# A 3x3 convolution of 16 images on one core: images paired across the partitions, and two output rows that share a product

## The chip, the cores and the metric

The kernel runs on one core of one Trainium2 chip. The metric is the device time of the kernel in microseconds (us), as the median of several runs. A profile of one execution goes with it: what each engine did and when, and what the DMA engines moved. The engines are TensorE (PE in the profile; its loads of weights are listed apart as PEld), VectorE (DVE), ScalarE (ACT), GpSimd (POOL) and SyncE (SP), whose only work here is to issue transfers.

## What is computed

The input `x` has 16 images of 64 channels and 64 x 64 pixels, the weight 128 output channels by 64 input channels by 3 x 3, both in fp32. The output is the convolution with a border of zeros, in fp32, 128 channels per image:

```python
x_pad = np.pad(x, ((0, 0), (0, 0), (1, 1), (1, 1)))
for b, co, ci, kh, kw in all_indices:          # 16, 128, 64, 3, 3
    if weight[co, ci, kh, kw] != 0:
        output[b, co] += weight[co, ci, kh, kw] * x_pad[b, ci, kh:kh+64, kw:kw+64]
```

Nine tenths of the weights are zero, at random places. Neither kernel makes use of it: both multiply with the full 64 x 128 matrix of each of the nine taps. The input is 16.8 MB, the output 33.6 MB.

## The kernel before

Each image is cut into an upper and a lower half of 32 rows. The 64 channels of the upper half lie in partitions 0 to 63, those of the lower half in 64 to 127, each with one more row at the cut (33 rows), so that the row is loaded twice. Loads are issued by GpSimd and turn fp32 into bf16 on the way. Images 1 to 14 are loaded two at a time.

```python
xs_group = xg_pool.tile([128, 2, XROWS, W], BF16, name="xsg")      # 3 buffers; XROWS = 33
nc.gpsimd.dma_start(                                                # line 107
    out=xs_group[0:64]...,   in_=x[b : b + 2, :, 0:XROWS, :]...)
nc.gpsimd.dma_start(                                                # line 111
    out=xs_group[64:128]..., in_=x[b : b + 2, :, H - XROWS : H, :]...)
```

A unit is 8 rows of the upper half and the same 8 of the lower one. For each of the nine taps there are two matmuls, one for each half: 64 channels against 8 x 64 pixels, with a 64 x 128 weight. The two use different rows of the array and different PSUM tiles. The nine taps add up in PSUM, and the sum is copied to SBUF by VectorE or ScalarE.

```python
for ui, (ur0, rb) in enumerate(units):
    ...                                       # psums: one [128, rb, 64] fp32 tile for each half
    for idx, (kh, kw) in enumerate(POS_ORDER):          # nine taps
        for half in range(2):
            ...                               # rows and columns of this tap, cut at the border
            nc.tensor.matmul(                           # line 175
                psum_t[:, rel_lo:rel_hi, j_lo:j_hi],
                wT[pbase : pbase + 64, kh * KW + kw, :],
                xs[idx_rhs],
                start=(idx == 0), stop=(idx == len(POS_ORDER) - 1),
            )
    if not streamed:
        for half in range(2):
            nc.any.tensor_copy(out=oimg[:, r0:r1, :], in_=psums[half])     # line 186
    else:                                     # images 13 to 15
        nc.vector.tensor_copy(...)                      # line 188
        nc.scalar.copy(...)                             # line 191
        ...                                   # store of these rows, 512 KB
```

Images 2 to 11 are stored in pairs of 4 MB, images 0, 1 and 12 alone, and images 13 to 15 unit by unit. The weights come in fp32, are cast to bf16 by VectorE, and are transposed with 18 matmuls against an identity (line 84).

Of the kernel before, what the change touches and what calls it, by code (L numbers as in the profile page):

```python
# [1 line left out]

# [5 lines left out]

FP32 = mybir.dt.float32  # L10
BF16 = mybir.dt.bfloat16


POS_ORDER = [(1, 1), (1, 0), (1, 2), (0, 0), (0, 1), (0, 2), (2, 0), (2, 1), (2, 2)]
CHUNK_ORDER = [1, 0, 2]


@with_exitstack
def kernel(
# [6 lines left out]
    nc = tc.nc  # L26

    B, C_IN, H, W = x.shape
    C_OUT, C_IN2, KH, KW = weight.shape
    assert (C_IN, H, W) == (64, 64, 64) and (C_OUT, KH, KW) == (128, 3, 3)  # L30

    HALF = H // 2
    XROWS = HALF + 1
    SPLIT = 10

    SINGLE_OUT = {0, 1, 12}
    PAIR_OUT_START = {2, 4, 6, 8, 10}
    STREAM_OUT = {13, 14, 15}
    UNITS_8 = [(r, 8) for r in range(0, HALF, 8)]
    STREAM_UNITS = {  # L40
        13: UNITS_8,
        14: UNITS_8,
        15: [(0, 8), (8, 8), (16, 8), (24, 4), (28, 4)],
    }

    const_pool = ctx.enter_context(tc.tile_pool(name="const", bufs=1))
    x0_pool = ctx.enter_context(tc.tile_pool(name="x0", bufs=2))
    xg_pool = ctx.enter_context(tc.tile_pool(name="xg", bufs=3))
    outs_pool = ctx.enter_context(tc.tile_pool(name="osb", bufs=3))
    outg_pool = ctx.enter_context(tc.tile_pool(name="osbg", bufs=2))  # L50
    psum_pool = ctx.enter_context(tc.tile_pool(name="psum", bufs=8, space=bass.MemoryType.PSUM))

    xs0 = x0_pool.tile([128, XROWS, W], BF16, name="xs0")
    nc.gpsimd.dma_start(out=xs0[0:64, 0:SPLIT], in_=x[0, :, 0:SPLIT, :])  # L54
    nc.gpsimd.dma_start(  # L55
        out=xs0[64:128, 0:SPLIT], in_=x[0, :, H - XROWS : H - XROWS + SPLIT, :]
    )
    nc.gpsimd.dma_start(out=xs0[0:64, SPLIT:XROWS], in_=x[0, :, SPLIT:XROWS, :])  # L58
    nc.gpsimd.dma_start(  # L59
        out=xs0[64:128, SPLIT:XROWS], in_=x[0, :, H - XROWS + SPLIT : H, :]  # L60
    )

    w_sb = const_pool.tile([C_OUT, C_IN * KH * KW], FP32)
    nc.sync.dma_start(out=w_sb, in_=weight.rearrange("o i kh kw -> o (i kh kw)"))
    w_sb3 = w_sb.rearrange("o (i k) -> o i k", k=KH * KW)

    w_bf = const_pool.tile([C_OUT, C_IN * KH * KW], BF16)
    w_bf3 = w_bf.rearrange("o (i k) -> o i k", k=KH * KW)
    for kh in CHUNK_ORDER:
        nc.vector.tensor_copy(  # L70
            out=w_bf3[:, :, kh * KW : (kh + 1) * KW],
            in_=w_sb3[:, :, kh * KW : (kh + 1) * KW],
        )

    ident = const_pool.tile([128, 128], BF16)
    make_identity(nc, ident)

    wT = const_pool.tile([128, KH * KW, C_OUT], BF16)
    for kh in CHUNK_ORDER:
        wps = psum_pool.tile([128, 4, 128], FP32, name="psum_t")  # L80
        for j in range(KW):
            sl = w_bf3[:, :, kh * KW + j]
            for half in range(2):
                nc.tensor.matmul(  # L84
                    wps[half * 64 : (half + 1) * 64, j, :],
                    sl,
                    ident,
                    start=True,
                    stop=True,
                )  # L90
        nc.scalar.copy(out=wT[:, kh * KW : kh * KW + KW, :], in_=wps[:, 0:KW, :])  # L91

    xs_group = None
    oimg_pair = None

    for b in range(B):
        if b == 0:
            xs = xs0
            xsel = ()
        elif b == B - 1:  # L100
            xs = x0_pool.tile([128, XROWS, W], BF16, name="xs15")
            nc.gpsimd.dma_start(out=xs[0:64], in_=x[b, :, 0:XROWS, :])  # L102
            nc.gpsimd.dma_start(out=xs[64:128], in_=x[b, :, H - XROWS : H, :])  # L103
            xsel = ()
        elif b % 2 == 1:
            xs_group = xg_pool.tile([128, 2, XROWS, W], BF16, name="xsg")
            nc.gpsimd.dma_start(  # L107
                out=xs_group[0:64].rearrange("i n r c -> i n (r c)"),
                in_=x[b : b + 2, :, 0:XROWS, :].rearrange("n i r c -> i n (r c)"),
            )  # L110
            nc.gpsimd.dma_start(  # L111
                out=xs_group[64:128].rearrange("i n r c -> i n (r c)"),
                in_=x[b : b + 2, :, H - XROWS : H, :].rearrange(
                    "n i r c -> i n (r c)"
                ),
            )
            xs = xs_group
            xsel = (0,)
        else:
            xs = xs_group  # L120
            xsel = (1,)

        if b in SINGLE_OUT or b in STREAM_OUT:
            oimg = outs_pool.tile([C_OUT, H, W], FP32, name="oimg")
        elif b in PAIR_OUT_START:
            oimg_pair = outg_pool.tile([C_OUT, 2, H, W], FP32, name="oimg2")
            oimg = oimg_pair[:, 0]
        else:
            oimg = oimg_pair[:, 1]

        streamed = b in STREAM_OUT
        if streamed:
            oimg_blk = oimg.rearrange("o (blk r) c -> o blk r c", blk=2)
            out_blk = out[b].rearrange("o (blk r) c -> o blk r c", blk=2)
            units = STREAM_UNITS[b]
        else:
            units = UNITS_8

        for ui, (ur0, rb) in enumerate(units):
            psums = []  # L140
            infos = []
            for half in range(2):
                r0 = half * HALF + ur0
                r1 = r0 + rb
                start_row = 0 if half == 0 else H - XROWS
                pbase = half * 64
                psum_t = psum_pool.tile([128, rb, W], FP32, name="psum_t")
                psums.append(psum_t)
                infos.append((r0, r1, start_row, pbase))

            for idx, (kh, kw) in enumerate(POS_ORDER):
                di, dj = kh - 1, kw - 1
                for half in range(2):
                    r0, r1, start_row, pbase = infos[half]
                    psum_t = psums[half]

                    i_lo = max(r0, -di)
                    i_hi = min(r1, H - di)
                    j_lo = max(0, -dj)
                    j_hi = min(W, W - dj)  # L160

                    rel_lo, rel_hi = i_lo - r0, i_hi - r0
                    xr_lo = i_lo + di - start_row
                    xr_hi = i_hi + di - start_row
                    xc_lo, xc_hi = j_lo + dj, j_hi + dj

                    idx_rhs = (slice(pbase, pbase + 64),) + xsel + (
                        slice(xr_lo, xr_hi),
                        slice(xc_lo, xc_hi),
                    )  # L170
                    rhs = xs[idx_rhs]
                    out_ap = psum_t[:, rel_lo:rel_hi, j_lo:j_hi]
                    lhsT = wT[pbase : pbase + 64, kh * KW + kw, :]

                    nc.tensor.matmul(  # L175
                        out_ap,
                        lhsT,
                        rhs,
                        start=(idx == 0),
                        stop=(idx == len(POS_ORDER) - 1),  # L180
                    )

            if not streamed:
                for half in range(2):
                    r0, r1, _, _ = infos[half]
                    nc.any.tensor_copy(out=oimg[:, r0:r1, :], in_=psums[half])  # L186
            else:
                nc.vector.tensor_copy(  # L188
                    out=oimg[:, infos[0][0] : infos[0][1], :], in_=psums[0]
                )  # L190
                nc.scalar.copy(  # L191
                    out=oimg[:, infos[1][0] : infos[1][1], :], in_=psums[1]
                )
                src = oimg_blk[:, :, ur0 : ur0 + rb, :]
                dst = out_blk[:, :, ur0 : ur0 + rb, :]
                if ui % 2 == 0:
                    nc.sync.dma_start(out=dst, in_=src)
                else:
                    nc.scalar.dma_start(out=dst, in_=src)  # L199

        if b in SINGLE_OUT:
            nc.sync.dma_start(out=out[b], in_=oimg)
        elif (b - 1) in PAIR_OUT_START:
            nc.sync.dma_start(
                out=out[b - 1 : b + 1].rearrange("n o h w -> o n (h w)"),
                in_=oimg_pair.rearrange("o n h w -> o n (h w)"),
            )


# [28 lines left out]
```

## Time and profile before

| | |
|---|---|
| time, median of 3 runs | 137.39 us (137.11 to 138.22) |
| span of the profiled execution | 136.1 us |
| moved by DMA, as it lands | 42.67 MB |
| read from HBM | 17.60 MB |
| written to HBM | 33.55 MB |
| instructions of TensorE | 1188 matmuls, 1188 loads of weights |

In the profile, a group of instructions is written as line, engine, operation, what it writes, `<-`, what it reads, with the shapes, the count, the total busy time and the mean time of one in ns. After the second bar stands how long the engine sat idle just before these instructions, and what it then had waited for. Rows of digits cut the span into 40 equal slices; a 9 means 90% busy or more. "DMA" in such a row is the mean busy share of the core's 16 DMA engines. The busy times of matmuls overlap, since two run at once. L175 is line 175 of the kernel, and the same line serves all products of the convolution.

### The profile page before, as it was taken

The page shows a single profiled execution, that of the slowest core. Times are in us where ns is not written, and L with a number is a line of the kernel's source. Part 1 is how long each engine was busy: PE and PEld are TensorE (multiplying, and loading weights), DVE is VectorE, ACT ScalarE, POOL GpSimd, SP SyncE. Part 2 cuts the span into 40 slices and gives each one's busy share as a digit, 9 for nine tenths or more (in the row PEclk, how much of TensorE's full clock was granted, in tenths as well). Part 3 has the DMA queues.
Part 4 walks back from the last instruction along what each step waited for, and adds up shares of the span by engine and source line. Part 5 has one row for each costly group of instructions (what it writes and reads, how often), then busy time and mean ns, then how long its engine had stood idle before and what let it go on. Part 6 is the DMA issues. An engine that isn't in the chain of part 4 may idle for free.

```text
span 136.1 us, 2653 instructions
## 1 busy us (share of the span) xinstructions
PE 126.7 (93%) x1188; PEld 77.1 (57%) x1188; DVE 45.2 (33%) x68; ACT 40.2 (30%) x69; POOL 12.2 (9%) x26
## 2 busy tenths in 40 slices
PE   0699999999999999999999999999999999999960
PEld 0555666666565656665656655665656655656650
DVE  0203432344234432343234423443244333443240
ACT  3302332233323332233223332333233323332230
POOL 6950000003000110003000110000000000000000
PEclk9999999999999999999999999999999999999999
DMA  4999999999999999999999999999509999999884
GB/s 104 119 189 211 216 229 350 363 342 363 245 226 409 443 338 195 302 416 443 274 205 393 438 395 228 294 405 455 231 10 462 385 453 409 389 404 393 329 326 157
DMA packets 7980, 42.67 MB, mean 313 GB/s; under 512 B 673, under 2 KB 1313, under 8 KB 6305
## 3 DMA queue, kind: packets, MB, share of 16 engines
q1 hardware_dynamic: 3840, 30.97, 55.6%
q0 software_dynamic: 2496, 8.65, 33.4%
q10 hardware_dynamic: 1632, 2.88, 5.6%
q8 instruction: 9, 0.15, 0.4%
q14 instruction: 3, 0.02, 0.0%
HBM read 17.60 MB, written 33.55 MB: 376 GB/s over the span
## 4 chain that ended last, share of the span: by engine, by line
PE 92%; POOL 2%; issue 1%; ACT 1%; ACTq 0%; POOLq 0%
PE psum_t L175 91%; PE psum_t L84 1%; ACT oimg L191 1%; POOL xs L54 0%; ACTq L199 0%; POOL xs L55 0%; POOL xsg L107 0%; POOL xs L58 0%; POOL ident masks.py:199 0%; POOL ident masks.py:197 0%; POOL xs L59 0%; POOLq masks.py:199 0%; POOLq L222 0%
## 5 line engine op out<-in xcount | busy, mean ns | idle before, releaser
L175 PE MATMUL psum_t<-xsg,wT 64*128 64x512 bf16 (+2 forms) x1008 | 108.1, 374 | 0.0
L175 PEld LDWEIGHTS <-wT 64*128 64x128 bf16 x1170 | 75.8, 95 | 49.6 <-issue 1.9
L186 DVE COPY oimg<-psum_t 128x512 f32<-128x512 f32 x52 | 36.0, 692 | 68.6 <-PE psum_t L175 68.6
L186 ACT COPY oimg<-psum_t 128x512 f32<-128x512 f32 x52 | 30.5, 586 | 71.7 <-PE psum_t L175 71.7
L175 PE MATMUL psum_t<-xs,wT 64*128 64x504 bf16 (+5 forms) x162 | 18.0, 378 | 0.0
L188 DVE COPY oimg<-psum_t 128x512 f32<-128x512 f32 (+1 forms) x13 | 8.5, 650 | 14.3 <-PE psum_t L175 14.3
L191 ACT COPY oimg<-psum_t 128x512 f32<-128x512 f32 (+1 forms) x13 | 7.2, 554 | 16.0 <-PE psum_t L175 16.0
L107 POOL DMA_DIRECT2D xsg<-in_x_dram x7 | 4.2, 599 | 64.4 <-PE psum_t L175 64.4
L84 PE MATMUL psum_t<-ident,w_bf 128*64 128x128 bf16 x18 | 1.3, 321 | 4.7 <-POOL ident masks.py:199 4.7
L111 POOL DMA_DIRECT2D xsg<-in_x_dram x7 | 4.2, 607 | 0.0
L84 PEld LDWEIGHTS <-w_bf 128*64 128x64 bf16 x18 | 1.3, 208 | 4.5 <-DVE w_bf L70 4.1
L91 ACT CAST wT<-psum_t 128x384 bf16<-128x384 f32 x3 | 1.2, 487 | 3.3 <-PE psum_t L84 3.3
L70 DVE CAST w_bf<-w_sb 128x192 bf16<-128x192 f32 x3 | 0.8, 345 | 3.7 <-DMA w_sb<-in_weight_dram 3.7
L91 ACT ACT_TABLE_LOAD x1 | 1.3, 1283 | 0.7 <-PEq L222 0.7
L54 POOL DMA_DIRECT2D xs<-in_x_dram x1 | 0.7, 659 | 0.8 <-POOLq L222 0.8
L102 POOL DMA_DIRECT2D xs<-in_x_dram x1 | 0.5, 527 | 0.9 <-DMA xs<-in_x_dram 0.9
L103 POOL DMA_DIRECT2D xs<-in_x_dram x1 | 0.5, 522 | 0.4 <-DMA xs<-in_x_dram 0.4
L59 POOL DMA_DIRECT2D xs<-in_x_dram x1 | 0.6, 554 | 0.0
L55 POOL DMA_DIRECT2D xs<-in_x_dram x1 | 0.5, 542 | 0.0
L58 POOL DMA_DIRECT2D xs<-in_x_dram x1 | 0.5, 542 | 0.0
masks.py:199 POOL TENSOR_SCALAR_AFFINE_SELECT ident<-ident 128x128 bf16<-128x128 bf16 x1 | 0.4, 397 | 0.1
masks.py:197 POOL MEMSET ident<- 128x128 bf16 x1 | 0.3, 266 | 0.0
(4 smaller groups left out, 0.4 us busy)
## 6 DMA issues: line engine op xcount, KB each, us to landing
out_dram<-oimg SPq DMA_DIRECT2D x5, 4096.0 KB, 14.3
xsg<-in_x_dram POOLq DMA_DIRECT2D x14, 528.0 KB, 10.5
out_dram<-oimg SPq DMA_DIRECT2D x3, 2048.0 KB, 12.3
out_dram<-oimg SPq DMA_DIRECT2D x6, 512.0 KB, 7.0
out_dram<-oimg ACTq DMA_DIRECT2D x5, 512.0 KB, 6.8
xs<-in_x_dram POOLq DMA_DIRECT2D x2, 264.0 KB, 27.3
xs<-in_x_dram POOLq DMA_DIRECT2D x2, 184.0 KB, 6.0
w_sb<-in_weight_dram SPq DMA_DIRECT2D x1, 288.0 KB, 3.0
```

What stands on the lines that cost most here:

```text
L54: nc.gpsimd.dma_start(out=xs0[0:64, 0:SPLIT], in_=x[0, :, 0:SPLIT, :])
L55: nc.gpsimd.dma_start(out=xs0[64:128, 0:SPLIT], in_=x[0, :, H - XROWS : H - XROWS + SPLIT, :])
L59: nc.gpsimd.dma_start(out=xs0[64:128, SPLIT:XROWS], in_=x[0, :, H - XROWS + SPLIT : H, :])
L70: nc.vector.tensor_copy(out=w_bf3[:, :, kh * KW : (kh + 1) * KW], in_=w_sb3[:, :, kh * KW : (kh + 1) * KW],)
L84: nc.tensor.matmul(wps[half * 64 : (half + 1) * 64, j, :], sl, ident, start=True, stop=True,)
L91: nc.scalar.copy(out=wT[:, kh * KW : kh * KW + KW, :], in_=wps[:, 0:KW, :])
L107: nc.gpsimd.dma_start(out=xs_group[0:64].rearrange("i n r c -> i n (r c)"), in_=x[b : b + 2, :, 0:XROWS, :].rearrange("n i r c -> i n (r c)"),
L111: nc.gpsimd.dma_start(out=xs_group[64:128].rearrange("i n r c -> i n (r c)"), in_=x[b : b + 2, :, H - XROWS : H, :].rearrange("n i r c -> ...
L175: nc.tensor.matmul(out_ap, lhsT, rhs, start=(idx == 0), stop=(idx == len(POS_ORDER) - 1),)
L186: nc.any.tensor_copy(out=oimg[:, r0:r1, :], in_=psums[half])
L188: nc.vector.tensor_copy(out=oimg[:, infos[0][0] : infos[0][1], :], in_=psums[0])
L191: nc.scalar.copy(out=oimg[:, infos[1][0] : infos[1][1], :], in_=psums[1])
```

## The change

The kernel is written anew around the same convolution.

- **Pairs of images.** The two images of a pair lie one above the other in the 128 partitions, so that two matmuls side by side belong to two images and not to two halves of one. No row is loaded twice. All eight pairs have their own tile and stay in SBUF.
- **Two rows share a product.** With G0, G1, G2 for the three rows of the weight, an even output row r is G0 x[r-1] + G1 x[r] + G2 x[r+1], and the row below is G0 x[r] + G1 x[r+1] + G2 x[r+2]. Both contain G1 (x[r] + x[r+1]) if the rest is corrected: the even row is that plus G0 x[r-1] + (G2 - G1) x[r+1], the odd row is that plus (G0 - G1) x[r] + G2 x[r+2]. GpSimd adds the rows, ScalarE copies the shared product to SBUF, and VectorE adds it to the two other sums when it takes them out of PSUM. Five row weights are kept in place of three. The first 16 rows of the first pair are computed directly.
- **Start.** The first 32 rows of the first pair come in fp32 on the queue of SyncE behind the weights, and are cast by VectorE and ScalarE. The transposes are 9 matmuls in place of 18, and give each weight to both halves of the partitions. TensorE runs 14 matmuls on zeros, 7 before the transposes and 7 after.
- **Loads and stores.** Pairs 1 to 3 and 24 rows of pair 4 are loaded at once; the rest is issued by GpSimd between its adds. Images are stored whole, 2 MB each, by SyncE; those of the last pair in two parts of 1 MB. After the second pair SyncE also issues four loads of one number each into a spare tile.

The instructions are issued in the order in which they are written (`manual_schedule`).

The diff, cut to its core:

```diff
-    xs_group = xg_pool.tile([128, 2, XROWS, W], BF16, name="xsg")     # halves of an image, 33 rows
+    xs = [x_pool.tile([128, H, W], BF16, name=f"x{p}") for p in range(NP)]     # NP = 8 pairs
+    def pair(p):
+        return x[2 * p : 2 * p + 2].rearrange("n i h w -> (n i) h w")
     nc.sync.dma_start(out=w_sb, in_=weight...)
+    nc.sync.dma_start(out=x_head[:, 0:HEAD, :], in_=pair(0)[:, 0:HEAD, :])     # HEAD = 32, fp32
+    nc.gpsimd.dma_start(out=xs[0][:, HEAD:H, :], in_=pair(0)[:, HEAD:H, :])
+    def load(p, a=0, b=H):
+        nc.gpsimd.dma_start(out=xs[p][:, a:b, :], in_=pair(p)[:, a:b, :])
+    EARLY, CUT = 4, 24
+    LATER = {2: (5,), 3: (6,), 4: (7, 0, 32), 5: (7, 32, 64)}
+    for p in range(1, EARLY):
+        load(p)
+    load(EARLY, 0, CUT)
+    keep_busy(7)                                  # matmuls on zeros; 7 more after the transposes
 ...
+    def product(terms, rows):
+        ps = [psum_pool.tile([128, rows, W], FP32, name="ps") for _ in range(2)]
+        todo = [(t, kw) for t in terms for kw in KW_ORDER]
+        for i, ((src, g, first, step), kw) in enumerate(todo):
+            ...                                   # rows a:b:step and columns, cut at the border
+            for n in range(2):                    # the two images of the pair
+                nc.tensor.matmul(ps[n][...], tap(g, kw, n), src[64*n : 64*n+64, a:b:step, ...],
+                                 start=(i == 0), stop=(i == len(todo) - 1))
+        return ps
 ...
+    def twos(p, o, r0):                           # 16 output rows of two images
+        s = s_pool.tile([128, 8, W], BF16, name="s")                  # 3 buffers
+        nc.gpsimd.tensor_tensor(out=s, in0=xs[p][:, r0 : r0 + 16 : 2, :],
+                                in1=xs[p][:, r0 + 1 : r0 + 16 : 2, :], op=ADD)
+        shared = product([(s, G1, 0, 1)], 8)
+        pc = []
+        for n in range(2):
+            c = p_pool.tile([128, 8, W], FP32, name="pc")             # 4 buffers
+            nc.scalar.copy(out=c, in_=shared[n])
+            pc.append(c)
+        even = [(xs[p], G21, r0 + 1, 2), (xs[p], G0, r0 - 1, 2)]
+        odd = [(xs[p], G01, r0, 2), (xs[p], G2, r0 + 2, 2)]
+        for first, terms in ((r0, even), (r0 + 1, odd)):
+            ps = product(terms, 8)
+            for n in range(2):
+                nc.vector.tensor_tensor(out=o[n][:, first : r0 + 16 : 2, :],
+                                        in0=ps[n], in1=pc[n], op=ADD)
 ...
-    for b in range(B):                            # units of nine taps; stores of one or two images
+    for p in range(NP):
+        o = [o_pool.tile([C_OUT, H, W], FP32, name="o") for _ in range(2)]     # 7 buffers
+        for blk in range(4):
+            ...                                   # direct for block 0 of pair 0, else twos(p, o, 16 * blk);
+                                                  # after block 3 the load that LATER names (pair 1: rest of pair 4);
+                                                  # last pair: stores of 32 rows after blocks 1 and 3
+        if not last:
+            for n in range(2):
+                nc.sync.dma_start(out=out[2 * p + n], in_=o[n])
+        if p == 1:
+            for k in range(4):
+                nc.sync.dma_start(out=spare[:, k : k + 1], in_=weight[0:1, 0, 0, 0:1])
```

## The prediction

> **What bounds the kernel now.** I began with the page: busy shares, clock and DMA rows, then the chain of work that ended last, then the groups by line.
>
> ```profile
> PE 126.7 (93%) x1188; PEld 77.1 (57%) x1188; DVE 45.2 (33%) x68; ACT 40.2 (30%) x69; POOL 12.2 (9%) x26
> PEclk9999999999999999999999999999999999999999
> DMA  4999999999999999999999999999509999999884
> ...
> PE 92%; POOL 2%; issue 1%; ACT 1%; ACTq 0%; POOLq 0%
> ...
> L175 PE MATMUL psum_t<-xsg,wT 64*128 64x512 bf16 (+2 forms) x1008 | 108.1, 374 | 0.0
> ...
> L186 DVE COPY oimg<-psum_t 128x512 f32<-128x512 f32 x52 | 36.0, 692 | 68.6 <-PE psum_t L175 68.6
> L186 ACT COPY oimg<-psum_t 128x512 f32<-128x512 f32 x52 | 30.5, 586 | 71.7 <-PE psum_t L175 71.7
> ```
>
> TensorE holds 92% of the chain, its product line has idle 0.0, and the eviction engines wait for it. So TensorE is the bound. But the DMA row says 9 nearly throughout: the DMA engines are almost full too, merely not last. A change that takes a sixth off TensorE can run into them. So I asked for stretches with one kind of traffic each (columns: stretch, its length, the five engines' busy time with counts, clock, DMA share, GB/s landed):
>
> ```profile
> 10.00:19.00 9.00, 9.00 (x88) 5.42 (x86) 3.46 (x5) 2.83 (x5) 0.00 (x0) 1.00 1.06 214
> 21.00:27.00 6.00, 6.00 (x60) 3.61 (x57) 2.07 (x3) 1.76 (x3) 0.00 (x0) 1.00 1.01 354
> 74.00:80.00 6.00, 6.00 (x60) 3.62 (x58) 2.32 (x4) 1.86 (x4) 1.17 (x2) 1.00 1.01 432
> ```
>
> 10 to 19 is image loads alone: 214 GB/s, counted as the bf16 that lands (twice that in fp32 is read). 74 to 80 is stores alone: 432 GB/s. 21 to 27 is a mixture. Its packets are 67 GB/s of loads and 290 of stores; 67/214 + 290/430 = 0.99. So the two costs simply add: **4.7 us per MB of bf16 loaded, 2.33 us per MB stored** (taking 430).
>
> For the pace of the products: a kernel matmul has 64 rows of weights, and two run side by side. Between 30 and 98 us the windows view counts 637 weight loads in 68 us, so a side-by-side couple takes 2 x 68/637 = 0.2135 us.
>
> **What the Trainium skill says.** "VectorE: DVE Perf Modes", section "The perf-mode tier table": a two-tensor operation with an operand in PSUM runs at one element per cycle. The trace has no such operation, but its copies out of PSUM take 692 ns for 512 elements and 424 for 256, 1.05 ns per element, so I give the new adds 0.69 us each. "SBUF — State Buffer", "Who interferes with whom": a VectorE instruction with one SBUF input does not contend with GpSimd; the new VectorE adds read one operand from PSUM and one from SBUF. No row here shows it. "GPSIMD Engine Reference", "Elementwise — side-by-side cycle accounting": an fp32 add of 2048 elements took 4497 ns; a quarter is an estimate of 1.1 us for 512; no row here shows it. "DMA: Bandwidth & Descriptors", "Where 436 GB/s comes from": 435 GB/s is the fabric's ceiling. The trace agrees: 432 in stores, 428 read in loads. I take this as a wall that the change cannot move.
>
> **TensorE, step by step.** Before: 16 images x 4 units x 9 taps = 576 couples. After: a block of 16 rows of an image pair needs 3 couples for the shared product, 6 for even rows and 6 for odd rows, 15 against 18. One block of 32 stays direct: 31 x 15 + 18 = 483 couples. 483 x 0.2135 = 103.1 us. At the top and bottom edge both halves of a couple now lose the missing row together (before only one of two did): 8 pairs x 6 couples x 1/8 x 0.2135 = 1.3 us less. That leaves **101.8 us**, against the chain's 124.5 on the same line: 22.7 us off.
>
> Start: products began at 5.9 us before, but a couple took about 0.42 us until 9.6 (timeline), a loss of 1.8 us; the new filler matmuls should have spent that slow phase. Against that, the first rows now come as 1.05 MB in fp32, behind 0.29 MB of weights, sharing the engines with the first loads: 1.05 MB at some 215 GB/s is 4.9 us from about 2.4, then a cast. I choose 8.0 us for the first product, an estimate. TensorE ends at 8.0 + 101.8 = 109.8, two adds bring 111.2.
>
> **VectorE, ScalarE, GpSimd.** A block takes TensorE 15 x 0.2135 = 3.2 us. VectorE has 4 adds, 4 x 0.69 = 2.8 us; ScalarE 2 copies of 0.586, 1.2 us; GpSimd one add, about 1.1. All fit beside TensorE, VectorE with 0.4 us to spare. Of the eight PSUM tiles a block takes six; a tile comes round again after more than a block's time less its own product, so I expect no TensorE wait while VectorE keeps under 3.2 us.
>
> **DMA, step by step.** Stores: 16 x 2.097 = 33.55 MB, unchanged, x 1/430 = 78.0 us. Loads cast on the way: 8 pairs x 1.049 MB bf16 less the half pair that comes as fp32, 7.86 MB; at 0.214 MB/us 36.7 us. (The 33rd row that both halves read is gone: 0.26 MB or 1.2 us.) Fp32 head and weights, 1.05 + 0.29 MB at 430: 3.1 us. Sum **117.8 us of DMA time**, 16 us more than TensorE's 101.8; its earlier start gives back about 6 of these.
>
> Is it one unbroken stretch? Early loads are 4.06 MB, 19.0 us; with head and weights DMA has work from 1.7 us (first weight packet before) to 24. The first pair is ready at about 8.0 + 63 x 0.2135 + 1.4 = 23, just in time. From there each pair brings 9.75 us of stores every 12.8 us, and the other 3.8 MB of loads, 17.8 us, fill the difference. Walking that forward, stores fall behind and DMA still has 5 to 10 us of queued work when TensorE stops. So DMA never idles and **takes TensorE's place as bound**. Losses: between 9.5 and 96.5 us the old packets carry 7.73 MB of loads and 20.65 MB of stores, worth 84.3 of those 87 us; 3% was lost where traffic changed kind. I allow 2.5 us for all of it, including a less patchy start.
>
> The end: the last old packet ended at 134.7, the span at 136.1: 1.5 us. Span: 1.7 + 117.8 + 2.5 + 1.5 = 123.5. The measured median stood 1.3 above the profiled span (137.39 against 136.1), so **124.8 us**, 9% below.
>
> **The rivals.**
>
> 1. TensorE stays the bound. 111.2, then the last 2.1 MB of stores in 4.9 us, 0.5 us of issue and 1.5 of end: span 118, time 119.5. Its support is today's chain; against it stands the DMA sum, which would have to be 6 us too large although both rates are measured.
> 2. VectorE becomes the bound. If reading PSUM and SBUF together, or the row-strided output, made an add 1.0 us, 124 adds would be 124 us, plus 12 us of start and 7 of end: some 144 us, slower than before. For it: the adds are 87% of TensorE's block time and no row shows one. Against it: copies run at exactly one element per ns or so. I give it 4%.
> 3. DMA bound, with starvation: a load takes only 67 of 214 beside stores, so 1.05 MB then needs 16 us. Pair 5 is issued near 37 us and needed at 72, pair 6 near 49 and needed at 85, the second half of pair 7 near 75 and needed at 104. If GpSimd, which issues loads between its adds, falls behind, TensorE stops, the queue drains and the end moves to 128 to 132.
> 4. Output tiles short. Seven tiles of one image: pair 7 needs the first store of pair 4 landed by 97; I have it near 86. Slack 10 us, so hidden.
>
> **Range and chances.** Without any loss the DMA sum gives 121.0 + 1.3 = 122.3; with somewhat faster stores 121.5. With starvation 130. So 121.5 to 130 for eight in ten. Over 2% faster means below 134.6: 0.93. Within 2%: 0.04, slower: 0.03, both mostly rival 2.
>
> **What would show it.** DMA share near 1.0 from 3 to 122 us with no gap near 24 us; TensorE's last product near 110 with more than 10 us of stores after it; VectorE's adds near 0.69 us; the last 1 MB stores waiting much longer than 5 us from issue to landing. Wrong if the add is over 0.8 us, if TensorE waits for loads or PSUM, if DMA has holes, or if stores run well away from 430 GB/s.

## The result and the profile after

The changed kernel takes 126.4 us (median), the one before 137.4: a ratio of 0.918 with a 95% interval of 0.916 to 0.921. Predicted were 124.8 us, with 121.5 to 130 as the range. The first profiled execution of the changed kernel was disturbed (130.17 us); the lines below are those of a second profiled run of the same kernel (run `again`, 126.61 us, span 124.5).

From the page and the list of groups by line: busy shares, TensorE and DMA over 40 slices, and the groups.

```profile
PE 109.8 (88%) x989; PEld 49.7 (40%) x989; DVE 82.4 (66%) x135; ACT 38.9 (31%) x71; POOL 41.6 (33%) x47
...
PE   6999999999999999999999999999999999960000
...
DMA  4999999999999999999999999999999999999991
...
L150 PE MATMUL ps<-x,wT 64*128 64x504 bf16 (+3 forms) x780 | 88.3, 373 | 0.0
L183 DVE TENSOR_TENSOR o<-ps,pc 128x512 f32<-128x512 f32 x124 | 77.8, 685 | 22.1 <-PE ps L150 19.8 <-ACT pc L176 2.3
...
L169 POOL TENSOR_TENSOR s<-x 128x512 bf16<-128x512 bf16 x31 | 35.5, 1149 | 57.5 <-PE ps L150 41.6 <-issue 12.2 <-ACT x L101 3.7
L176 ACT COPY pc<-ps 128x512 f32<-128x512 f32 x62 | 33.3, 589 | 64.0 <-issue 61.8 <-PE ps L150 2.2
```

TensorE is still dense from about 3 to 111 us, with no wait in front of its products, but its row now ends four slices before the span does, while the DMA row is full to the last slice. From the chain, in order of time (start, duration, what):

```profile
7.82 102.04 PE ps L150 x954
109.86 0.01 DVEq L183
...
111.80 0.60 DVE o L183
```

The chain leaves TensorE at 109.9 us, when the sums for the even rows of the last block are done; the last products, in the second line of TensorE's timeline below, end at 108.35 + 2.68 = 111.0:

```profile
107.70 0.81 PE L150 MATMUL ps<-s,wT 64*128 64x512 bf16 x6
108.35 2.68 PE L150 MATMUL ps<-x,wT 64*128 64x512 bf16 x24
```

The chain follows compute instructions and ends with the last add, at 112.4, 12 us before the span's end. What fills these 12 us stands in the list of transfers (count, size of each, median time from issue to landing):

```profile
out_dram<-o SPq DMA_DIRECT2D x14, 2048.0 KB, 16.8
x<-in_x_dram POOLq DMA_DIRECT2D x5, 1024.0 KB, 16.1
out_dram<-o SPq DMA_DIRECT2D x4, 1024.0 KB, 11.9
```

A store of 1 MB takes 2.4 us at 430 GB/s; the last four need 11.9 from issue to landing, because they queue. That is what a bound by transfers looks like here: the chain by engines ends early, and the transfers behind it are old when they start.

### The profile page after: what moved, and what is told of

Read it like the earlier page. It is cut to its first block, busy times and chain, and to the rows that moved or that the text cites. A ratio compares the mean times of both kernels' runs of the same rounds, so it can differ in the third digit from the quotient of the medians.

```text
span 127.2 us, 2468 instructions
## 1 busy us (share of the span) xinstructions
PE 111.3 (87%) x989; PEld 57.9 (46%) x989; DVE 82.4 (65%) x135; ACT 38.9 (31%) x71; POOL 41.7 (33%) x47
## 3 DMA queue, kind: packets, MB, share of 16 engines
q0 software_dynamic: 1440, 7.86, 30.0%
## 4 chain that ended last, share of the span: by engine, by line
PE 82%; DMA 6%; DVE 1%; issue 1%; DVEq 0%; SPq 0%
PE ps L150 82%; DMA o<-in_x_dram 6%; DVE o L183 1%; DVEq L242 0%; DVE x L101 0%; SPq L60 0%; DVEq L183 0%
## 5 line engine op out<-in xcount | busy, mean ns | idle before, releaser
L150 PE MATMUL ps<-x,wT 64*128 64x504 bf16 (+3 forms) x780 | 90.5, 379 | 2.3 <-DVE x L101 2.3
L183 DVE TENSOR_TENSOR o<-ps,pc 128x512 f32<-128x512 f32 x124 | 77.8, 685 | 22.1 <-PE ps L150 19.8
L150 PEld LDWEIGHTS <-wT 64*128 64x128 bf16 x966 | 55.3, 95 | 52.0 <-issue 4.7
L169 POOL TENSOR_TENSOR s<-x 128x512 bf16<-128x512 bf16 x31 | 35.6, 1151 | 61.2 <-PE ps L150 42.7
L176 ACT COPY pc<-ps 128x512 f32<-128x512 f32 x62 | 33.3, 589 | 64.0 <-issue 61.8
L150 PE MATMUL ps<-s,wT 64*128 64x512 bf16 (+1 forms) x186 | 25.7, 377 | 0.0
L86 PE MATMUL ps<-idle_rhs 128*128 128x512 bf16 x14 | 5.5, 562 | 1.2 <-DVE idle_rhs L81 1.2
L68 POOL DMA_DIRECT2D x<-in_x_dram x9 | 5.0, 560 | 0.0
L86 PEld LDWEIGHTS <-idle_rhs 128*128 128x128 bf16 x14 | 1.8, 136 | 3.6 <-issue 2.2
L101 ACT CAST x<-o 128x576 bf16<-128x576 f32 (+1 forms) x2 | 1.5, 802 | 3.5 <-DMA o<-in_x_dram 3.5
L63 POOL DMA_DIRECT2D x<-in_x_dram x1 | 0.7, 693 | 0.8 <-POOLq L231 0.8
## 6 DMA issues: line engine op xcount, KB each, us to landing
x<-in_x_dram POOLq DMA_DIRECT2D x1, 640.0 KB, 15.4
```

What stands on the lines that cost most here:

```text
L68: nc.gpsimd.dma_start(out=xs[p][:, a:b, :], in_=pair(p)[:, a:b, :])
L86: nc.tensor.matmul(idle_ps, idle_rhs[:, 0:128], idle_rhs, start=True, stop=True)
L101: copy(out=xs[0][:, a:b, :], in_=x_head[:, a:b, :])
L150: nc.tensor.matmul(ps[n][:, lo:hi, c_lo:c_hi], tap(g, kw, n), src[q, a:b:step, c_lo + kw - 1 : c_hi + kw - 1], start=(i == 0), stop=(i == ...
L169: nc.gpsimd.tensor_tensor(out=s, in0=xs[p][:, r0 : r0 + 16 : 2, :], in1=xs[p][:, r0 + 1 : r0 + 16 : 2, :], op=ADD)
L176: nc.scalar.copy(out=c, in_=shared[n])
```

## The experiments

Eleven runs, of which the first repeats the changed kernel. Ratios are against the kernel before, run on the same chip. "The changed kernel" is 126.5 us in this comparison (run `again`). Runs 5 to 8 and 9 to 11 were on two other chips, where the kernel before took 137.4 us and not 137.9 and the changed kernel itself was not run; so a few tenths of a us more or less than 126.5 mean little there.

**1. The same kernel again.**

> The changed kernel once more, unchanged, for a second profile. In the first profile DMA stood idle from about 24.2 to 26.5 us, because the first products began at 9.8 us (8.0 was expected) and ran slowly until 13.4. Theory 1 (DMA sets the end): where the products begin or speed up earlier this hole is smaller, and the span shrinks by just as much: about 124.5 us with a hole under 0.5 us. Theory 2 (TensorE sets the end): the span follows the end of the products with a fixed rest of about 11 us, whatever DMA's hole is.

126.5 us, ratio 0.916 (0.914 to 0.919), span 124.5. Products began at 7.8 us and ended at 111.0; DMA had no hole. The chain's end at 112.4 and the rest of 12 us don't tell the theories apart alone, so the next three do.

**2. A third of the products.**

```diff
-KW_ORDER = (1, 0, 2)
+KW_ORDER = (1,)
```

> Leaves out two of the three columns of the weights, so that each sum has a third of its products; transfers, adds and copies are as they were. TensorE's products fall from 103 to about 35 us; VectorE's 124 adds (85 us) then set the pace of the blocks. Theory 1 (DMA sets the end): stores come a little earlier, the hole near 24 us goes, and nothing else changes: span 121.5 to 123 us, time 123 to 124.5. Theory 2 (TensorE, through its products and what follows them): the last add at about 98 us, and span near 107.

126.1 us (ratio 0.914, 0.912 to 0.916), span 124.4: two thirds of TensorE's work left out, and 0.4 us gained. From its page (TensorE, then DMA over the 40 slices) and its groups of waits:

```profile
PE   6987888778977878866101989388874000000000
...
DMA  4999999999999999999999999999999999999991
```

```profile
L183 DVE TENSOR_TENSOR o<-ps,pc 128x512 f32<-128x512 f32 x124 | 74.7, 678 | 13.8 <-DMA out_dram<-o 11.6 <-PE ps L150 2.1
```

TensorE now has holes, and VectorE waits 11.6 us for output tiles that have not been stored yet. Its last add ends at 98.6 us, as Theory 2 had it, but the span lasts 26 us longer. Compute is idle, DMA is not, and the time stays. This settles which resource sets the end. It also shows a miss: I had expected 123 to 124.5 us. So 126.1 is about what the transfers need, 1.3 us more than the prediction's 124.8.

**3. A few of the stores.**

```diff
-nc.sync.dma_start(out=out[2 * p + n], in_=o[n])
+nc.sync.dma_start(out=out[2 * p + n][:, 0:8, :], in_=o[n][:, 0:8, :])
-rows = slice(r0 - 16, r0 + 16)              # last pair
+rows = slice(r0 + 8, r0 + 16)
```

> Stores 8 rows where the changed kernel stores 64 (8 rows of each 32 in the last pair), so that most of the output stays unwritten; 29 of 33.6 MB of stores are gone, all computation stays. Theory 1 (DMA sets the end): TensorE's own time shows: products end at about 110 to 113.5 us as before, and the span is about 2.5 to 3.5 us more than that, 114 to 117, time 115.5 to 118.5. Theory 2 (TensorE sets the end): the span shrinks by no more than the 4.9 us of the last stores and stays above 119.

116.9 us, span 115.0, as Theory 1 had it. Products ended at 110.6, and DMA now has the holes:

```profile
PE   5999999999999999999999999999999999999940
...
DMA  4999999999703794079702940078000400002204
```

So the new kernel needs 117 us for its computation and 126 for its transfers; without these 29 MB of stores it is 9.6 us faster.

**4. Nine taps for every block.**

```diff
-BLOCKS = {p: "TTTT" for p in range(8)}
-BLOCKS[0] = "DTTT"
+BLOCKS = {p: "DDDD" for p in range(8)}
```

The later loads are moved out of the branch of the shared product, so that they are still issued.

> Computes every block directly with nine taps, as the old kernel did, inside the new kernel's pairs, loads and stores (the loads all go early, since GpSimd has no adds between them). 576 couples of products in place of 483, 19.9 us more for TensorE: products end at about 131 to 133 us, then the last 2.1 MB of stores. Theory 1: TensorE is now the later one by far and DMA waits for it: span 138 to 140, time 139 to 141, so the shared product is worth 13 to 15 us of the 20 that it takes off TensorE. Rival (the gain comes from layout, loads and stores and not from the shared product): time stays near 126 to 130.

141.9 us, ratio 1.032 (1.027 to 1.037), span 139.7: slower than the kernel before, and 15.4 us slower than with the shared product. Its products end at 130.7, 0.7 us before those of the old kernel (131.4); but then 2.1 MB remain to be stored, where the old kernel had stored its last images 512 and 256 KB at a time. The windows view from the end of the products to the last transfer (columns as in the prediction: stretch, length, engines, clock, DMA share, GB/s):

```profile
130.70:138.40 7.70, 0.00 (x0) 0.00 (x0) 0.69 (x1) 0.56 (x1) 0.00 (x0) 0.78 0.78 321
```

So the new layout by itself gains nothing, and loses 4 us to its coarser last stores: from the last product to the end of the span it takes 9.0 us, the old kernel 4.7. With the shared product the products end 19.7 us earlier (19.9 were expected), and 15.4 of them arrive.

**5 and 6. More work for TensorE, the same transfers.** One block, then two, of every pair directly.

```diff
+BLOCKS = {p: "DTTT" for p in range(8)}      # run 5
+BLOCKS = {p: "DDTT" for p in range(8)}      # run 6
```

> Computes the first 16 rows of every pair directly (before: of the first pair alone). 7 blocks of 18 couples in place of 15 add 21 couples, 4.5 us, to TensorE, which then ends at about 114.4 us in place of 109.9. Transfers are the same. Theory 1 (DMA is last, TensorE has slack): the last stores still wait in the queue, time 126.3 to 127.3, at most 0.8 us more. Theory 2 (TensorE sets the end): time 131.

> Computes the first 32 rows of every pair directly: 15 more blocks with 3 more couples each, 45 couples, 9.6 us more for TensorE, which then ends at about 119.5 us. The last two 1 MB stores can't begin before about 121 and need 5 us and 1.5 of end. Theory 1 (slack of about 5 to 6 us in TensorE): the slack is used up and the rest shows: span 127 to 128.5, time 129 to 130.5, 2.5 to 4 us more. Theory 2 (TensorE sets the end): time 136.

128.4 and 133.3 us. Products end at 115.4 and 120.8, so 4.4 and 9.7 us were added and 1.9 and 6.8 arrived: a slack of 2.5 to 2.9 us, about half of what I had expected. The loss is not at the end. Windows of run 5, then of run 6:

```profile
102.60:103.60 1.00, 1.00 (x14) 0.53 (x10) 0.73 (x2) 0.00 (x0) 0.00 (x0) 1.00 0.35 147
```

```profile
92.70:94.10 1.40, 1.40 (x18) 0.76 (x15) 1.21 (x3) 0.00 (x0) 0.00 (x0) 1.00 0.20 82
104.20:108.20 4.00, 4.00 (x42) 2.21 (x40) 3.09 (x6) 1.07 (x2) 0.00 (x0) 1.00 0.02 8
```

DMA runs dry (shares 0.35, 0.20, 0.02) before the stores of the last but one pair, which are issued only when the whole image is done, and with two direct blocks before those of pair 5 as well. By the packets these holes are 5.5 of the 6.6 us by which the span of run 6 grew, but only 0.7 of the 2.0 us of run 5. Another 1.0 us of run 5 is lost from 15 to 30 us, for a reason that stays open; there the rest of pair 4 was issued at 20.0 us in place of 23.3, because GpSimd had fewer adds in front of it. Counted by the holes alone, TensorE's slack is about 4 us. It is the smallest lead of the queue over all stores, not the queue behind the last one.

**7. The fp32 rows in two transfers.**

```diff
-nc.sync.dma_start(out=x_head[:, 0:HEAD, :], in_=pair(0)[:, 0:HEAD, :])
+for a, b in ((0, 9), (9, HEAD)):
+    nc.sync.dma_start(out=x_head[:, a:b, :], in_=pair(0)[:, a:b, :])
```

> The 32 fp32 rows at the start are loaded in two transfers, 9 rows and then 23, so that the first cast and the first products wait for 0.29 MB and not for 1.05 MB. The products should begin near 6 us in place of 7.8 and end near 108.5. Theory 1: the end is DMA's, so time stays within 0.4 us of the changed kernel's 126.5. Theory 2 (TensorE sets the end): 1.5 us less, 125.

132.3 us, 5.8 more, which neither theory had. The first 9 rows did come early, but the products began only at 7.6 us, behind the weights' transposes and the filler matmuls, and stopped from 9.6 to 13.9 for the other 23 rows; after that a couple took 0.42 us until about 17, and 0.21 from there on. The packets of the 23 rows start at 4.5 us, after GpSimd's loads (3.8), and from there alternate with them until 12.0; in the changed kernel the packets of the fp32 rows start at 2.6, before the loads (5.4), and the last starts at 5.7. TensorE's stop made the first store late (issued at 28.0 us in place of 22.2), and DMA ran out of early loads:

```profile
9.70:13.80 4.10, 0.00 (x0) 0.00 (x0) 0.68 (x1) 0.64 (x2) 0.00 (x0) 0.96 1.07 233
25.20:28.70 3.50, 3.50 (x38) 1.83 (x34) 2.55 (x5) 1.42 (x4) 1.49 (x2) 1.00 0.06 11
```

From 25.2 to 28.7 us DMA is idle (0.06) while TensorE is at full pace. Against run 1, by the packets, 4.0 us of DMA work more are lost from 25 to 35 us and 0.7 before 10, and the span grows by 5.0. My expectation was wrong in its premise, an earlier start, but the span grew by about what DMA lost.

**8. All loads at the start.**

```diff
-EARLY, CUT = 4, 24
-LATER = {2: (5,), 3: (6,), 4: (7, 0, 32), 5: (7, 32, 64)}
+EARLY, CUT = 7, 64
+LATER = {}
```

> All loads are issued at the start, none between the adds. The bytes are the same. Theory 1 (DMA's sum sets the end, and its order doesn't matter as long as there is work): time within 0.6 us of 126.5, at best a little less since no hole can come before the first store. Rival (the placing of loads among stores is itself worth something: early stores slowed by loads would hold the output tiles, and TensorE would wait): TensorE shows waits for output tiles and time grows by 2 us or more.

127.3 us, ratio 0.927 (0.923 to 0.931) against 0.916: 0.8 us more, slightly outside what either theory had. Products still ran from 7.9 to 111.2 us without a wait; the output tiles were not short.

**9. Less of the output stored.**

```diff
-nc.sync.dma_start(out=out[2 * p + n], in_=o[n])
+nc.sync.dma_start(out=out[2 * p + n][:, 0:60, :], in_=o[n][:, 0:60, :])
-rows = slice(r0 - 16, r0 + 16)              # last pair
+rows = slice(r0 - 16, r0 + 14)
```

> Stores 60 of the 64 rows of each image (30 of each 32 in the last pair); the other rows of the output stay unwritten, and all computation stays. 2.1 MB of stores less are 4.9 us of DMA time at 430 GB/s. Theory 1 (the sum of the transfers sets the end): about 4.5 us less, near 122.0 us. Theory 2 (TensorE and the stores that follow it set the end): only the last 2.1 MB are 1/16 shorter, 0.3 us less, 126.2.

122.6 us, 3.9 less; span 120.4, 4.1 less. TensorE did the same work (products to 110.8). A sixteenth of the stores moves the end by most of the 4.9 us; about 1.2 us of DMA work are missing from 95 to 100 us, where shorter stores ran ahead of the computation.

**10 and 11. Variants of the start.** A smaller fp32 head, and all of pair 4 at the start.

```diff
-HEAD = 32
+HEAD = 18                                   # run 10, without the cast of rows 18 to 31
-EARLY, CUT = 4, 24
+EARLY, CUT = 4, 64                          # run 11, without the later load of pair 4
```

> Loads 18 rows in place of 32 of the first pair as fp32 behind the weights; the other 46 come with GpSimd's first load. One transfer, as in the changed kernel, of 0.59 MB. The DMA sum is the same. The products should begin near 6.7 us in place of 7.8 and, unlike with the head in two transfers, not stop again, since the 46 rows are first in their queue and needed near 11 us. Theory 1: time within 0.4 us of 126.5 where the changed kernel has no hole. Theory 2: 1.1 us less. If the 46 rows come late (after 11 us) the products stop, a hole follows near 24 us, and the time grows by as much as the hole is long.

> All of pair 4 is loaded at the start, where the changed kernel loads its first 24 rows then and the other 40 between the adds of pair 1. That is 3.1 us more of early work for DMA, so that the first store may come up to 3 us later without a hole; bytes are the same. Theory 1: where the first store is in time anyway, nothing changes: within 0.5 us of 126.5. If the placing itself matters (loads beside stores cost more or less than their sum), it shows here as a change of the sum.

126.1 us (ratio 0.917, 0.914 to 0.920) and 126.9 (0.922, 0.919 to 0.925). Run 10 began its products at 7.0 us, stopped for 0.3 us at 11 (the 46 rows landed just late), had no hole, and takes the time of the changed kernel. Run 11 lies between the changed kernel and run 8, so moving loads to the start seems to cost a little, though 0.4 us is close to what executions of one kernel differ by; why, is open. None of these variants of start and loads beats the changed kernel clearly. No run leaves out the matmuls on zeros or the four loads of one number, so what these are worth is not shown.

## Why the prediction was right, and what it had wrong

**DMA takes TensorE's place as bound: right, and shown.** Leaving out products changes 0.4 us (run 2), leaving out stores changes 3.9 to 9.6 (runs 9 and 3), and of 4.4 us of added products only 1.9 arrive (run 5).

**TensorE's side: right, but for one deduction.** I had 8.0 us for the first product, 101.8 for all, 109.8 for the end of the last and 111.2 for the last add; measured are 7.8, 103.3, 111.0 and 112.4. Two adds came after the last product, as I had counted. What was wrong are the 1.3 us that I took off for the rows at the border: the pace of 0.2135 us, an average over the old trace, had such rows in it already, and the new kernel has the same pace with its own (638 loads of weights from 30 to 98 us, against 637). Without the deduction my sum was 103.1. The saving on TensorE is real, but 9.6 us of it lie under the transfers.

**VectorE and GpSimd: right.** The add from PSUM and SBUF takes 685 ns against 0.69 us estimated, so rival 2 falls; the GpSimd add takes 1149 ns against 1.1. VectorE's idle time is nearly all spent on TensorE's products (19.8 us). In run `again` TensorE waits for no later load and no engine for an output tile, so rivals 3 and 4 did not come about either.

**The DMA sum: right.** The packets of run `again` carry 7.86 MB of loads and 34.9 MB of stores, weights and fp32 rows, at 214 and 430 GB/s 117.9 us of work, against 117.8. The mixture costs the sum of its parts, as read from the old trace. Two windows, of loads and stores mixed and of stores alone:

```profile
24.00:100.00 76.00, 76.00 (x716) 34.80 (x714) 59.56 (x96) 25.75 (x48) 29.41 (x28) 1.00 1.02 374
100.00:112.00 12.00, 11.03 (x104) 4.81 (x100) 9.64 (x16) 3.24 (x7) 0.20 (x1) 1.00 1.00 425
```

Both are full (shares 1.02 and 1.00) at 374 and 425 GB/s. In the first, the packets carry 4.0 MB of loads and 24.3 of stores, 74.9 us of work in 76.

**The losses: too small, and this is most of the error.** I allowed 2.5 us; the packets give 3.6: 0.8 in the first 5 us beside the 1.7 until the first packet, 1.3 from there to 120 us, and 1.5 at the very end, which I had not counted. The last packets end at 123.2 but the engines do not stop together:

```profile
119.00:120.50 1.50, 0.00 (x0) 0.00 (x0) 0.00 (x0) 0.00 (x0) 0.00 (x0) 0.50 1.03 437
120.50:121.50 1.00, 0.00 (x0) 0.00 (x0) 0.00 (x0) 0.00 (x0) 0.00 (x0) 0.50 0.74 311
121.50:122.50 1.00, 0.00 (x0) 0.00 (x0) 0.00 (x0) 0.00 (x0) 0.00 (x0) 0.50 0.27 115
122.50:123.50 1.00, 0.00 (x0) 0.00 (x0) 0.00 (x0) 0.00 (x0) 0.00 (x0) 0.50 0.08 33
```

With 1.3 us from the last packet to the end (1.5 predicted), 1.7 + 117.9 + 3.6 + 1.3 = 124.5, the span; predicted were 123.5.

**From span to time: mis-sized too.** I added 1.3 us, from a median and a profile that are not of one execution. Taken run by run, time is about 1.8 us above the span before and about 2.0 after. That is the other 0.6 of the 1.6 us between 124.8 and 126.4.

**The backlog: 5 to 10 us were predicted when TensorE stops.** At 111.0 us the packets still to come are 10.6 us of DMA work, 4.9 of them not yet issued: 5.7 are queued, at the low end. But this is not TensorE's slack, as I treated it afterwards: that was 2.5 to 2.9 us by the times of runs 5 and 6, and about 4 by the holes.

## What to carry to other kernels

Add up the bytes of each kind of transfer at the rates that the old trace shows for it alone, and set the sum beside the engine that you relieve: a nearly full DMA row says nothing while another engine ends last, and sets the time once that one is faster. The larger of the two sums then sets the time, and further relief of the engine is worth next to nothing (0.4 us for two thirds of the products here). In such a kernel protect the queue: it must have work from the first packet, and every store must be issued before the one in front of it ends.

## What the runs showed of the hardware

- Two transfers of one queue are not served in one piece when another queue starts between them: in run 7 the packets of the second took from 4.5 to 12.0 us beside GpSimd's loads, for 0.75 MB.
- The DMA engines drift apart over a long unbroken stretch. In runs 1, 8, 10 and 11 the 16 closing packets of the last store, taken as one for each engine, come over 2 to 3 us. After a hole shortly before the end they come together, apart from one: in run 6, after the hole at 104 to 108 us, 15 had come by 128.4 and the last came at 129.9. One 16 KB instruction fetch of 0.9 us lay between that hole and the end, which would fit one late engine; but no run took the fetches away, and in run 4, where one engine is late too, the fetch lies before the last hole.
- Moving loads from later to the start went with 0.4 us more (run 11, hardly more than noise) and 0.8 us more (run 8), with TensorE waiting for none of them. By the packets the loss lies at 25 to 30 us, where early loads end and first stores begin. With 0.54 to 0.58 MB of loads in these 5 us (runs 5, 6, 8 and 11) the DMA engines, busy throughout, do 0.6 to 0.8 us of work too little; with 0.13 to 0.26 MB (runs 1, 9 and 10), 0.0 to 0.2. The cause is open.
